# Making the decay matrices' rectified differences during attention and loading them in the state-space stage of a hybrid decoder block

## The chip, the cores and the metric

The kernel runs on one core of a Trainium2 chip. The metric is the device time of one execution in microseconds (us), the median of several runs. The engines are named as in the profile: PE (TensorE, matrix products), PEld (its weight loads), DVE (VectorE), ACT (ScalarE), POOL (GpSimd), SP (SyncE, which issues most DMAs). Each engine takes its own instructions strictly in order; semaphores join the engines.

## The reference

One layer of a hybrid decoder, sequence 1024 with 16 meta tokens ahead, model width 1024. Three mixers read the same normalised input: stick-breaking attention (8 heads of 64), a Mamba-2 state-space mixer (16 heads of 64, state 128) and latent attention (MLA, 8 heads); their joined output is projected and added, and a gated feed-forward layer follows. The change touches the state-space mixer, which works in chunks of 128 tokens:

```python
dA = (dt * a).reshape(b, nc, BLOCK, G, J)
Acs = jnp.cumsum(dA, axis=2)
seg = Acs[:, :, :, None] - Acs[:, :, None, :]
Ldec = jnp.exp(jnp.where(tri[None, None, :, :, None, None], seg, -jnp.inf))
CB = jnp.einsum('bclgn,bcsgn->bclsg', Cc, Bc)
y_diag = jnp.einsum('bclsgj,bcsgjp->bclgjp', CB[..., None] * Ldec, X)
decay = jnp.exp(Acs[:, :, -1:] - Acs)
states = jnp.einsum('bclgn,bclgjp->bcgjpn', Bc, X * decay[..., None])
chunk_decay = jnp.exp(Acs[:, :, -1])
y_off = jnp.einsum('bclgn,bcgjpn->bclgjp', Cc, prev) * jnp.exp(Acs)[..., None]
```

The running sums `Acs` (one number for each token and head) are known long before the state-space stage; everything in the exponentials comes from them alone.

## The kernel before

Activations lie with features on the partitions. Products at full precision are made of three passes (high by high, high by low, low by high parts), lines L145 to L147. Up to about 460 us the kernel does stick-breaking attention in four pairs of heads; beside them, as filler for PE, it makes the next pair's projections and the units of the convolution (`conv_unit`). ACT takes the results out of PSUM (sigmoids `cm`, casts `ph`, `K`, `KS`, `Q`, `cacc`); the two PSUM banks of `d_ps` serve all filler.

In pair 1 the running sums are made (`running_sums`): the product `acum` with a triangular matrix gives `AT` (token on the partition; block and head in the row), and transposed copies are stored in `s_sum` (block, head, token).

The state-space stage (`ssd_chunk`, from about 463 us) goes over 9 chunks (0 is the meta tokens) and in each over two groups `g` of 8 heads. For a group:

- SP loads `R`, the 8 rows of `s_sum`, to all 128 partitions (L786, 512 KB, four buffers).
- ACT makes `cd` (the chunk's whole decay), 8 rectified differences `L = relu(AT - R)` (L795), `ea = exp(R)` in two halves of 64 partitions (L793), and `exp(-L)` (L804). DVE makes `dec` (L789), ACT its exponential (L799).
- POOL scales `X` by `dec` into `Xd` (L800), the state `S` by `cd` (L821), `xs` by the skip gain (L760) and adds `ea` to `y` (L834). DVE multiplies `L` by the masked product `cbm` (L809), `ea` by `yo` (L814), and adds to `S` and `y`.
- PE makes the transpositions `xtp` and `btp`, the products `cbp`, `yo` (old state, L813), `sps` (new state, L817) and `yd` (within the chunk, L829).

Filler for PE there are the units of the latent projections (`latent_units`, L145 to L147), and after these the value projection of MLA (nine blocks, L896 to L898).

What sets the order: the code is written unit by unit, and a list scheduler with its own estimate of durations puts each engine's instructions into one fixed order, in which an instruction that is written later may fill a place that it holds to be free. Buffers come from pools; a tile waits until the earlier user of its buffer is done. `high_priority` and `issue_after` move single blocks.

Of the kernel before, what the change touches and what calls it, by code (L numbers as in the profile page):

```python
# [11 lines left out]
F32 = mybir.dt.float32  # L12
# [47 lines left out]
def tile_hybrid_block(ctx: ExitStack, tc: tile.TileContext, a: dict):  # L60
# [37 lines left out]
    s_v = dram.tile([9, 128, 512], F32, name="s_v")  # L98
    s_sum = dram.tile([9, 16, 128], F32, name="s_sum")
    s_inv = dram.tile([MLA_HEADS, SEQ], F32, name="s_inv")  # L100

# [316 lines left out]

    dx = keep.tile([128, 9 * 16], F32, name="dx")

    def step_sizes():
# [43 lines left out]
    def running_sums(d1):  # L465
        NC = 9 * 16
        pt = tp.tile([128, 512], F32, tag="tp", name="acum")
        pe.matmul(pt[:, :NC], tri, d1, start=True, stop=True)
        dve.tensor_copy(AT.rearrange("p b h -> p (b h)"), pt[:, :NC])

        for i, (t0, n) in enumerate(CH_ALL):
# [5 lines left out]
            act.copy(acs[:, :n], pt[:16, :n])  # L477
            if i == 0:
                sp.dma_start(s_sum[0, :, :META], acs[:, :META])
            nb = min(3, n // 128)  # L480
# [199 lines left out]
    with ctx_sb as st:  # L680
# [20 lines left out]
        pms = meta_tiles(sbb)  # L701

        def sb_attend(p, proj, values):
            Q, K, KS = proj
            for h in range(2):
                for j in range(NQ // 2):
                    rows = [sb_row(Q[h], K[h], KS[h], 2 * j + e) for e in range(2)]
                    weighted_values(tp, pvp, sbb, j, rows, values[0], h, [x[p, 64 * h : 64 * (h + 1)] for x in (s_osbh, s_osbl)], pms[j % 2], values[1])
                    if p == 1 and h == 0 and j == 1:
                        with tc.issue_after(last_on(PE)), tc.issue_after(last_on(DVE)), tc.issue_after(last_on(ACT)):  # L710
                            running_sums(decay_steps())

        values = load_value_steps(sbv, sbb, 0)
# [28 lines left out]
    with ExitStack() as st:  # L742
        la = st.enter_context(tc.tile_pool(name="la", bufs=1, side="right", reuse_waits="tile"))
        p2_st = ExitStack()
        p2 = p2_st.enter_context(tc.tile_pool(name="p2", bufs=2, side="right", reuse_waits="tile"))
        yps = st.enter_context(tc.tile_pool(name="yps", bufs=4, space=PSUM, reuse_waits="tile"))
        dsk = p2.tile([128, 8], F32, bufs=1, name="dsk")
        sp.dma_start(dsk, a["d_skip"])
        S = [p2.tile([128, 512], F32, bufs=1, name=f"S{g}") for g in range(2)]

        def ssd_chunk(c):
# [26 lines left out]
            for g in range(2):  # L778
                gs = slice(512 * g, 512 * (g + 1))
                hs = slice(8 * g, 8 * g + 8)  # L780
                cd = p2.tile([128, 8], F32, tag="cd", name="cd")
                dec = p2.tile([128, 8], F32, tag="dec", name="dec")
                L = p2.tile([128, 8, 128], F32, tag="L", name="L")
                ea = p2.tile([128, 4, 128], F32, tag="yt", bufs=1, name="ea")
                R = p2.tile([128, 8, 128], F32, tag="R", bufs=4, name="R")
                sp.dma_start(R[:, :, :n], s_sum[c, hs, :n].partition_broadcast(128))  # L786
                if c < 8:
                    act.activation(cd, R[:, :, n - 1], AF.Exp)
                    dve.tensor_tensor(dec[:n], R[:n, :, n - 1], AT[:n, c, hs], op=ALU.subtract)  # L789
                if c > 0:  # L790
                    for e in range(2):
                        half = slice(64 * e, 64 * e + 64)
                        act.activation(ea[half], R[half, e::2, :], AF.Exp)  # L793
                    for h in range(8):
                        act.activation(  # L795
                            L[:, h, :], R[:, h, :], AF.Relu, scale=-1.0, bias=AT[:, c, 8 * g + h : 8 * g + h + 1]
                        )
                if c < 8:
                    act.activation(dec[:n], dec[:n], AF.Exp)  # L799
                    pool.tensor_tensor(  # L800
# [958 lines left out]
```

## Time and profile before

| | |
|---|---|
| Median of 3 runs | 1741.38 us (1738.69 to 1743.46) |
| Profiled execution | 1737.8 us, span 1736.0 us |
| PE busy | 1681.3 us (97%) |
| ACT, DVE, POOL busy | 844.6, 1154.7, 735.3 us |
| 213.7 to 285 us (71.3 us): PE, ACT busy | 70.23, 43.65 us |
| 469 to 591 us (122 us): PE, ACT, DVE, POOL busy | 113.35, 98.36, 89.82, 90.32 us |

The span goes from the first to the last instruction of the program. A row of a group gives line, engine, operation, tiles (out<-in), shapes and count; then the busy time in us and the mean of one in ns; then the engine's idle time just before and who ended it. A row with three numbers joined by slashes gives minimum, median and maximum of one in ns. A row of the table by stretches gives start:end, length, then for PE, PEld, DVE, ACT and POOL the busy time with the number of instructions, then the granted clock of TensorE, the DMA engines' share and GB/s.

### The profile page before, as it was taken

The numbers are of one execution on the slowest core, as the hardware profiler recorded it, in microseconds if no ns is written. First come the engines' busy times: TensorE is split into PE (matmuls) and PEld (weight loads), VectorE is DVE, ScalarE is ACT, GpSimd is POOL, SyncE is SP. The second block draws the span as 40 slices with busy tenths as digits, with TensorE's granted clock in tenths as the row PEclk, the third lists the DMA queues.
The fourth block names the chain that finished last, engine by engine and source line by source line (L and its number), as shares of the span: only waits on it lengthen the run. The fifth ranks groups of instructions, "written<-read, shape, count | busy, mean of one in ns | idle before, by whom it ended". The sixth has DMA issues, their size and how long they took to land.

```text
span 1736.0 us, 26095 instructions
## 1 busy us (share of the span) xinstructions
PE 1681.3 (97%) x9529; PEld 1471.2 (85%) x9529; DVE 1154.7 (67%) x1726; ACT 844.6 (49%) x1763; POOL 735.3 (42%) x525
## 2 busy tenths in 40 slices
PE   8899999999998999999999999999999999999998
PEld 7889999999987789998888878778888888878887
DVE  7677568778587544556576556966666666688644
ACT  7465466556577627776454325422222322343333
POOL 3544335243578447563231445635554555200012
PEclk9999999999999999999999999999999999999999
DMA  4222222122566655348222352222322233999602
GB/s 164 72 73 66 82 81 88 39 83 71 173 213 170 211 203 153 113 122 285 62 80 75 94 178 73 71 100 92 113 93 97 93 101 110 329 395 370 234 1 97
DMA packets 150133, 230.90 MB, mean 133 GB/s; under 512 B 27043, under 2 KB 86597, under 8 KB 150005
## 3 DMA queue, kind: packets, MB, share of 16 engines
q1 hardware_dynamic: 130608, 213.67, 38.1%
q10 hardware_dynamic: 19396, 15.56, 3.0%
q8 instruction: 75, 1.23, 0.3%
q14 instruction: 54, 0.43, 0.1%
HBM read 166.07 MB, written 63.10 MB: 132 GB/s over the span
## 4 chain that ended last, share of the span: by engine, by line
PE 72%; DVE 7%; DMA 6%; issue 2%; POOL 2%; ACT 1%; SPq 1%; DVEq 0%; ACTq 0%; POOLq 0%
PE d_ps L145 8%; PE d_ps L147 8%; PE d_ps L146 8%; PE b_ps L1269 7%; PE b_ps L1271 7%; PE b_ps L1270 7%; PE b_ps L1554 2%; PE b_ps L1555 2%; PE b_ps L1553 2%; PE ptg L326 2%; DMA raw<-in_w_down_dram 1%; PE pv L305 1%; PE ptg L328 1%; PE pv L304 1%; PE sc_ps L979 1%
## 5 line engine op out<-in xcount | busy, mean ns | idle before, releaser
L145 PE MATMUL d_ps<-hnh,whi 128*128 128x384 f32 (+6 forms) x744 | 246.5, 331 | 3.6 <-DVE KS L607 2.4
L147 PE MATMUL d_ps<-hnl,whi 128*128 128x384 f32 (+6 forms) x744 | 246.6, 331 | 0.0
L146 PE MATMUL d_ps<-hnh,wlo 128*128 128x384 f32 (+6 forms) x744 | 245.8, 330 | 0.0
L134 POOL TENSOR_TENSOR wlo<-wraw,whi 128x1024 fp32r<-128x1024 f32 (+1 forms) x57 | 137.3, 2408 | 200.7 <-ACT whi L132 200.2
L145 PEld LDWEIGHTS d_ps<-hnh,whi 128*128 128x128 f32 (+1 forms) x744 | 140.1, 188 | 7.8 <-ACT vs L582 1.7
L147 PEld LDWEIGHTS d_ps<-hnl,whi 128*128 128x128 f32 (+1 forms) x744 | 140.1, 188 | 3.1 <-issue 0.8
L146 PEld LDWEIGHTS d_ps<-hnh,wlo 128*128 128x128 f32 (+1 forms) x744 | 140.1, 188 | 2.3
L1270 PE MATMUL b_ps<-T,wl 128*128 128x512 f32 x352 | 139.1, 395 | 1.3 <-POOL wl L1101 1.3
L1271 PE MATMUL b_ps<-T,wh 128*128 128x512 f32 x352 | 138.7, 395 | 1.3 <-DVE T L1101 1.3
L1269 PE MATMUL b_ps<-T,wh 128*128 128x512 f32 x352 | 139.1, 396 | 0.0
L312 DVE TENSOR_TENSOR pl<-ptg,ph 128x512 fp32r<-128x512 f32 (+1 forms) x160 | 99.8, 628 | 53.1 <-ACT ph L311 51.9
L696 DVE TENSOR_TENSOR_SCAN cm<-cm,sb_mask 128x144 f32<-128x144 f32 (+3 forms) x64 | 107.5, 1687 | 29.1 <-issue 18.8
L1100 ACT CAST op<-raw 128x1024 fp32r<-128x1024 f32 x69 | 71.1, 1050 | 110.3 <-PE d_ps L1555 65.4
L1101 DVE TENSOR_TENSOR op<-raw,op 128x1024 fp32r<-128x1024 f32 x69 | 84.1, 1229 | 40.5 <-ACT op L1100 40.4
L311 ACT CAST ph<-ptg 128x512 fp32r<-128x512 f32 (+1 forms) x160 | 85.6, 542 | 44.2 <-PE ptg L328 23.4
L132 ACT CAST whi<-wraw 128x1024 fp32r<-128x1024 f32 (+1 forms) x57 | 58.8, 1032 | 68.8 <-PE d_ps L147 35.1
L1101 POOL TENSOR_TENSOR wlo<-raw,whi 128x1024 fp32r<-128x1024 f32 x18 | 45.0, 2499 | 109.7 <-ACT whi L1100 109.7
L1101 POOL TENSOR_TENSOR wl<-raw,wh 128x512 fp32r<-128x512 f32 x46 | 75.5, 1648 | 30.2 <-ACT wh L1100 30.2
L1107 POOL TENSOR_TENSOR tt<-tt 128x512 f32<-128x512 f32 (+1 forms) x8 | 8.1, 1015 | 187.6 <-ACT tt L1625 187.4
L1104 DVE TENSOR_TENSOR raw<-raw 128x512 f32<-128x512 f32 x58 | 58.5, 1016 | 42.0 <-DMA raw<-in_w_gate_dram 37.3
L1100 ACT CAST wh<-raw 128x512 fp32r<-128x512 f32 x88 | 53.2, 616 | 65.9 <-PE b_ps L1271 65.8
L1270 PEld LDWEIGHTS b_ps<-T,wl 128*128 128x128 f32 x352 | 66.5, 189 | 17.3 <-POOL wl L1101 1.6
(431 smaller groups left out, 5117.8 us busy)
## 6 DMA issues: line engine op xcount, KB each, us to landing
raw<-in_w_down_dram SPq DMA_DIRECT2D x99, 256.0 KB, 5.3
s_hops<-gs SPq DMA_DIRECT2D x63, 256.0 KB, 2.0
raw<-s_hops SPq DMA_DIRECT2D x63, 256.0 KB, 5.4
raw<-in_w_gate_dram SPq DMA_DIRECT2D x22, 512.0 KB, 3.7
raw<-in_w_up_dram SPq DMA_DIRECT2D x22, 512.0 KB, 4.3
R<-s_sum SPq DMA_DIRECT2D x16, 512.0 KB, 4.7
wraw<-in_w_o_dram SPq DMA_DIRECT2D x16, 512.0 KB, 3.7
wraw<-in_w_xbc_dram SPq DMA_DIRECT2D x12, 512.0 KB, 4.0
```

The source lines that it names most:

```text
L134: pool.tensor_tensor(lo[:, :cols], raw[:, :cols], f32(hi[:, :cols]), op=ALU.subtract)
L145: pe.matmul(ps[:m, :n], wh, mh, start=(kt == 0), stop=False)
L146: pe.matmul(ps[:m, :n], wl, mh, start=False, stop=False)
L147: pe.matmul(ps[:m, :n], wh, ml, start=False, stop=(kt == nkt - 1))
L311: act.copy(ph[:, :n], pt[:, :n])
L312: dve.tensor_tensor(pl[:, :n], pt[:, :n], f32(ph[:, :n]), op=ALU.subtract)
L696: dve.tensor_tensor_scan(rev, rev, sb_mask[:, T - n_all :][:, ::-1], 1.0, ALU.mult, ALU.max)
L1100: act.copy(hi, value)
L1101: eng.tensor_tensor(lo, value, f32(hi), op=ALU.subtract)
L1269: pe.matmul(banks[j], hi[:, ks], UH[u][k], start=start and k == 0, stop=False, skip_group_check=skip)
L1270: pe.matmul(banks[j], lo[:, ks], UH[u][k], start=False, stop=False, skip_group_check=skip)
L1271: pe.matmul(banks[j], hi[:, ks], UL[u][k], start=False, stop=stop and k == 3, skip_group_check=skip)
```

## The change

For each chunk but the meta one and each group a function `differences` loads the 8 rows of `s_sum` to all partitions, makes the 8 rectified differences in place (`rel`, two buffers) and stores them in a new DRAM tensor `s_rel` (16 x 512 KB). It is called in the attention of pairs 2 and 3, once after each query step. The state-space stage loads `L` from `s_rel` (four buffers instead of two) and has no `R` any more; it loads the rows for `ea` a second time, by themselves (two loads of 128 KB for a group), and makes their exponential in one instruction over 128 partitions. `cd` and `dec` no longer come from `R`: `running_sums` makes the blocks' whole sums by two more products, subtracts `AT`, and a single exponential at the start of the stage (`decay`) makes all of both. The meta block's sums aren't stored any more. A scratch region for DMA descriptors is halved from 4096 to 2048.

```diff
+    SUMS = keep.tile([128, 2, 9 * 16], F32, name="SUMS")
...
+        pt = tp.tile([128, 512], F32, tag="tp", name="asum")
+        pe.matmul(pt[:, :16], ones[:META], d1[:META, :16], start=True, stop=True)
+        pe.matmul(pt[:, 16:NC], ones, d1[:, 16:], start=True, stop=True)
+        dve.tensor_copy(SUMS[:, 0], pt[:, :NC])
+        pool.memset(SUMS[:, 1, :16], 0.0)
+        for rows, c in ((slice(0, META), slice(0, 16)), (slice(0, 128), slice(16, NC))):
+            dve.tensor_tensor(
+                SUMS[rows, 1, c], SUMS[rows, 0, c], AT.rearrange("p b h -> p (b h)")[rows, c], op=ALU.subtract
+            )
...
-            if i == 0:
-                sp.dma_start(s_sum[0, :, :META], acs[:, :META])
...
+        def differences(c, g):
+            d = sbb.tile([128, 8, 128], F32, tag="rel", name="rel")
+            sp.dma_start(d, s_sum[c, 8 * g : 8 * g + 8].partition_broadcast(128))
+            for h in range(8):
+                act.activation(
+                    d[:, h, :], d[:, h, :], AF.Relu, scale=-1.0, bias=AT[:, c, 8 * g + h : 8 * g + h + 1]
+                )
+            sp.dma_start(s_rel[c - 1, g], d.rearrange("p h t -> p (h t)"))
...
+                    if p > 1:
+                        differences(4 * (p - 2) + j + 1, h)
...
+        decay = p2.tile([128, 2, 9, 16], F32, bufs=1, name="decay")
+        act.activation(decay.rearrange("p e b h -> p e (b h)"), SUMS, AF.Exp)
...
-                cd = p2.tile([128, 8], F32, tag="cd", name="cd")
-                dec = p2.tile([128, 8], F32, tag="dec", name="dec")
-                L = p2.tile([128, 8, 128], F32, tag="L", name="L")
-                ea = p2.tile([128, 4, 128], F32, tag="yt", bufs=1, name="ea")
-                R = p2.tile([128, 8, 128], F32, tag="R", bufs=4, name="R")
-                sp.dma_start(R[:, :, :n], s_sum[c, hs, :n].partition_broadcast(128))
-                if c < 8:
-                    act.activation(cd, R[:, :, n - 1], AF.Exp)
-                    dve.tensor_tensor(dec[:n], R[:n, :, n - 1], AT[:n, c, hs], op=ALU.subtract)
+                cd, dec = decay[:, 0, c, hs], decay[:, 1, c, hs]
                 if c > 0:
+                    L = p2.tile([128, 8, 128], F32, tag="L", bufs=4, name="L")
+                    ea = p2.tile([128, 4, 128], F32, tag="yt", name="ea")
+                    sp.dma_start(L.rearrange("p h t -> p (h t)"), s_rel[c - 1, g])
                     for e in range(2):
                         half = slice(64 * e, 64 * e + 64)
-                        act.activation(ea[half], R[half, e::2, :], AF.Exp)
-                    for h in range(8):
-                        act.activation(
-                            L[:, h, :], R[:, h, :], AF.Relu, scale=-1.0, bias=AT[:, c, 8 * g + h : 8 * g + h + 1]
-                        )
+                        sp.dma_start(ea[half], s_sum[c, 8 * g + e : 8 * g + 8 : 2].partition_broadcast(64))
+                    act.activation(ea, ea, AF.Exp)
                 if c < 8:
-                    act.activation(dec[:n], dec[:n], AF.Exp)
```

How the fixed order of instructions changes, at three places.

ACT in attention, just after the running sums, before (`acs` are the transposed running sums, `pm` and `ph` casts of attention weights, `K` and `KS` of keys, `whi` of weights):

```order
L318 CAST pm<-ptm 16x256
L311 CAST ph<-ptg 128x512
L132 CAST whi<-wraw 128x1024
L311 CAST ph<-ptg 128x512
L604 CAST K<-d_ps 64x272
L605 CAST KS<-d_ps 64x272
L694 ACT_TABLE_LOAD
```

and now (line numbers of the changed kernel):

```order
L319 CAST pm<-ptm 16x256
L312 CAST ph<-ptg 128x512
L716 ACTIVATE rel<-rel,AT 128x128 x8
L312 CAST ph<-ptg 128x512
L613 CAST K<-d_ps 64x272
L614 CAST KS<-d_ps 64x272
L133 CAST whi<-wraw 128x1024
L703 ACT_TABLE_LOAD
```

The first lot of eight differences stands here, in pair 1, and the other fifteen follow it; the last lot stands so, among the results of the convolution:

```order
L501 ACTIVATE cacc<-d_ps,cb,cw 128x272
L716 ACTIVATE rel<-rel,AT 128x128 x8
L319 CAST pm<-ptm 16x256
L501 ACTIVATE cacc<-d_ps,cb,cw 128x384
L512 ACTIVATE csig<-cacc 128x272
```

That `cacc` is the one that starts at 285.7 us in the trace of before. Between the first and the last lot stand 91 other instructions of ACT.

SP between the stores of the running sums and the first conv weights, now (`rel<-s_sum` is the load of a lot, `s_rel<-rel` its store; the load of `w_sbq` before stood right behind the stores of `s_sum`):

```order
L491 DMA s_sum<-acs 16x2x128
L491 DMA s_sum<-acs 16x3x128
L714 DMA rel<-s_sum 128x1024
L491 DMA s_sum<-acs 16x3x128
L131 DMA wraw<-in_w_sbq_dram 128x1024
L404 DMA vlast<-s_vsb 64x8x1 x4
```

and some 20 rows on:

```order
L714 DMA rel<-s_sum 128x1024
L131 DMA wraw<-in_w_xbc_dram 128x1024
L719 DMA s_rel<-rel 128x1024 x2
L714 DMA rel<-s_sum 128x1024 x2
L719 DMA s_rel<-rel 128x1024 x2
L714 DMA rel<-s_sum 128x1024 x2
L131 DMA wraw<-in_w_xbc_dram 128x1024
```

Loads and stores of the two `rel` buffers stand in turn in the one queue of SP, with the weights of the next unit behind them.

PE at the end of the state-space stage, before (all nine blocks of the value projection stand ahead of the last `yd`):

```order
L896 MATMUL d_ps<-whi,lhi 128x512
L897 MATMUL d_ps<-whi,llo 128x512
L898 MATMUL d_ps<-wlo,lhi 128x512
L829 MATMUL yd<-L,X 64x128 x8
L145 MATMUL d_ps<-lhi,whi 128x272
```

and now (the meta block, 16x512, and one of the others stand ahead of it, seven behind):

```order
L909 MATMUL d_ps<-whi,lhi 128x512
L910 MATMUL d_ps<-whi,llo 128x512
L911 MATMUL d_ps<-wlo,lhi 128x512
L842 MATMUL yd<-L,X 64x128 x8
L826 MATMUL yo<-bc,S_5597 128x128 x4
L842 MATMUL yd<-L,X 64x128 x8
L909 MATMUL d_ps<-whi,lhi 128x512
L910 MATMUL d_ps<-whi,llo 128x512
```

At the stage's other end, 24 filler products of 128x384 that stood ahead of the first `xtp` now stand behind it.

More of the change, by code (lines that the diff above doesn't have):

```diff
@@ L99, in tile_hybrid_block @@
     s_sum = dram.tile([9, 16, 128], F32, name="s_sum")
+    s_rel = dram.tile([8, 2, 128, 1024], F32, name="s_rel")
     s_inv = dram.tile([MLA_HEADS, SEQ], F32, name="s_inv")
@@ L1747 @@
     }
-    nc = bacc.Bacc("TRN2", target_bir_lowering=False, num_devices=1, dynamic_dma_scratch_size=4096)
+    nc = bacc.Bacc("TRN2", target_bir_lowering=False, num_devices=1, dynamic_dma_scratch_size=2048)
     aps = {
```

## The prediction

> **What bounds the kernel now.** The page first: TensorE (PE) is busy for 97% of the span, no other engine for more than 67%, and in the chain that ended last it holds 72%.
>
> ```profile
> span 1736.0 us, 26095 instructions
> PE 1681.3 (97%) x9529; PEld 1471.2 (85%) x9529; DVE 1154.7 (67%) x1726; ACT 844.6 (49%) x1763; POOL 735.3 (42%) x525
> PE 72%; DVE 7%; DMA 6%; issue 2%; POOL 2%; ACT 1%; SPq 1%; DVEq 0%; ACTq 0%; POOLq 0%
> ```
>
> So an edit pays only where PE waits, and it costs wherever it makes PE wait. Next the table by stretches, for the two stages that the change touches (each engine's busy time with its instructions in brackets, then granted clock, DMA share, GB/s):
>
> ```profile
> 213.70:285.00 71.30, 70.23 (x467) 66.57 (x467) 50.36 (x75) 43.65 (x96) 27.16 (x21) 1.00 0.28 79
> 300.00:340.00 40.00, 40.00 (x251) 37.27 (x250) 28.52 (x40) 22.63 (x54) 12.85 (x7) 1.00 0.20 59
> 340.00:380.00 40.00, 40.00 (x276) 39.13 (x275) 30.19 (x47) 23.68 (x53) 17.99 (x14) 1.00 0.24 70
> 469.00:591.00 122.00, 113.35 (x828) 93.15 (x826) 89.82 (x118) 98.36 (x249) 90.32 (x66) 0.97 0.65 201
> 469.00:480.00 11.00, 9.99 (x74) 9.45 (x71) 5.66 (x11) 8.16 (x28) 6.42 (x5) 1.00 1.05 371
> 480.00:591.00 111.00, 103.36 (x755) 83.70 (x755) 84.16 (x108) 90.20 (x222) 83.90 (x61) 0.97 0.61 184
> ```
>
> Attention (213 to 460 us) is PE's own: busy 40.00 of 40, weight loads (PEld) 37 to 39 of 40. The state-space stage, 122 us from its first transposition to its last product, is not: PE is busy for 113.35 but its weight loads for only 93.15 (76%), because matmuls overlap and a busy PE hides short waits. There ACT (98.36), POOL (90.32) and DVE (89.82) are all at three quarters or more. If weight loads stood as dense as in attention, the stage would last about 93.15/0.97 = 96 us; some 26 us is the most that it can give back.
>
> **What leaves the state-space stage.** Groups by line:
>
> ```profile
> L795 ACT ACTIVATE L<-R,AT 128x128 f32<-128x128 f32 x128 | 39.4, 388 | 1.6 <-PE yd L829 1.6
> L793 ACT ACTIVATE ea<-R 64x512 f32<-64x512 f32 x32 | 20.0, 625 | 1.3 <-POOL y L834 1.1
> L788 ACT ACTIVATE cd<-R 128x8 f32<-128x8 f32 x16 | 3.3, 209 | 2.9 <-POOL S L821 1.6 <-DMA R<-s_sum 1.0
> L799 ACT ACTIVATE dec<-dec 128x8 f32<-128x8 f32 (+1 forms) x16 | 3.2, 204 | 15.4 <-DVE dec L789 15.4
> L789 DVE TENSOR_TENSOR dec<-R,AT x16: 147/840/1039, 470.8 to 558.3; 128x8 f32<-128x8 f32 x14, 16x8 f32<-16x8 f32 x2
> ```
>
> The 128 rectified differences (39.4 us; 0.31 us apiece when they follow each other), the small exponentials (3.3 + 3.2) and half of `ea` go: 16 of 128x512 instead of 32 of 64x512, the same 512 columns, so 16 x 0.625 = 10.0 instead of 20.0. ACT falls by 39.4 + 10 + 6.5 = 56, from 98 to 42 us. DVE loses `dec`, 10.7 us, and ACT its 15.4 us wait for it.
>
> **What stays** is POOL's chain and DVE's long product (minimum/median/maximum ns):
>
> ```profile
> L809 DVE TENSOR_TENSOR L<-L,cbm x16: 1207/1969/3451, 483.0 to 586.8; 128x1024 f32<-128x1024 f32 x16
> L834 POOL TENSOR_TENSOR y<-y,ea x16: 1266/1286/2267, 490.9 to 590.2; 128x512 f32<-128x512 f32 x16
> L821 POOL TENSOR_TENSOR S<-S,cd x14: 1037/1048/2041, 488.2 to 582.1; 128x512 f32<-128x512 f32 x14
> L800 POOL TENSOR_TENSOR Xd<-X,dec x16: 1034/1046/2024, 473.6 to 566.4; 128x512 f32<-128x512 f32 x14, 16x512 f32<-16x512 f32 x2
> L760 POOL TENSOR_TENSOR y<-xs,dsk x8: 1897/1898/1933, 471.8 to 580.2; 128x1024 f32<-128x1024 f32 x8
> ```
>
> An 8-column DVE subtraction takes 147 ns at best and 840 at the median, L809 1.21 and 1.97 us, and POOL's L821 now and then double: DVE operations with both inputs in SBUF and POOL's take turns. At the minima POOL's four lines are 20.3 + 14.5 + 16.5 + 15.2 = 66.5 us, L809 19.3, `dec` 2.4; with POOL's other work here, 90.32 less the four lines' busy 74.7, or 15.6, that is 104 us of taking turns in 122 (85%). Without `dec` 101 remain, so the stage can't get under about 101. I take 111 us, about midway between that and the 119 at which the turns would again be 85% full, because the second crowded engine (ACT) is gone: 11 us off the stage, from 3 to 21. [...]
>
> The DMA side is a smaller brake. The new `ea` loads add 16 x 256 KB = 4.2 MB; 184 GB/s at a share of 0.61 is 302 GB/s when full, so they are 14 us of all DMA engines on top of 0.65 x 122 = 79: 93 in 111. It holds, with longer landings, and is a reason not to take less than 111.
>
> **Not all 11 us count.** Products of other units fill PE in this stage, and the order of the change puts fewer among them: 24 products of 128x384 that stood ahead of the first transposition now follow it, and of the nine blocks of the value projection (six products of 128x512 each, L896 to L898) that all stood ahead of the last `yd`, seven follow it: 42 products. Their pace:
>
> ```profile
> 457.00:463.00 6.00, 6.00 (x36) 6.00 (x35) 0.42 (x1) 2.03 (x5) 1.75 (x2) 1.00 0.65 157
> 1200.00:1240.00 40.00, 40.00 (x173) 32.31 (x173) 26.11 (x31) 11.85 (x19) 20.09 (x13) 1.00 0.31 99
> ```
>
> 6.00/36 = 0.17 us for 384 columns, 40/173 = 0.23 for 512. The stage starts 24 x 0.17 = 4.1 us earlier in PE's work and leaves 42 x 0.23 = 9.7 us for later, 5.6 net. It gives back 11 - 5.6 = 5.4 us.
>
> **What attention has to take.** The 128 differences do not spread over the last two pairs. On ACT the order puts them between the cast `ph` at 213.7 us and the accumulator `cacc` at 285.7, in 16 lots of eight, with about 90 of ACT's other instructions between. In those 71.3 us ACT is busy for 43.65 (row above); 39.4 more makes 83.05, an overload of 11.75 us even if ACT never waited. PE needs ACT for every bank that it fills (casts of K, Q and `ph`, sigmoids, `cacc`), and engines work in order, so what ACT is late by reaches PE, less PE's lead. More is added by the loads and stores of `rel`:
>
> ```profile
> DMA to landing us min/median/max: 3.5/4.6/5.7
> wraw<-in_w_xbc_dram SPq DMA_DIRECT2D x3, 512.0 KB, 3.9
> s_y<-y ACTq DMA_DIRECT2D x7, 512.0 KB, 3.5
> 218.00 1.05 ACT L132 CAST whi<-wraw 128x1024 fp32r<-128x1024 f32 x1 [3.67 <-DMA wraw<-in_w_sbq_dram]
> ```
>
> The first line is the same broadcast of 512 KB in the state-space stage (`R`), the second a load of that size in attention, the third a store of it. `rel` has two buffers, so each turns once per load 4.1 + eight differences 2.5 + store 3.5 + issues 0.7 = 10.8 us: 5.4 per lot, 86 us for 16. ACT's own pace is 83.05/16 = 5.2 per lot. Two rings of equal pace, joined in order, hold each other up: I add 5 us, between 0 (ACT always finds its lot landed) and 15 (about one per lot). The first lot has to wait for the running sums to be stored and read back; ACT stood idle there anyway for 3.67 us, so 1 more. The load waits on SP, and behind it stand the queries' weights (the `whi` above waits for them), and later the conv weights and the stores of `csig`; on ACT a lot whose load is late holds the casts behind it, for which PE waits. Both are in the 5. PE's lead takes off 3, between 0 and 6: two banks of 24 products of 0.17 us. The two sums by matmul, three DVE operations and a memset are 0.5 (0 to 1.5): they follow the copy of `AT` in DVE's queue and nothing reads them before the state-space stage. Attention: 11.75 + 5 + 1 - 3 + 0.5 = 15 us, between 6 and 28. It isn't won back, for PE has no idle time behind it until 465.
>
> Costed at nothing: the loads of `L`, which have the size of those of `R`, and four buffers as these had. They are freed later, by `yd` instead of the differences, still two chunks ahead. If that cover went, a landing of 4.6 us per lot would show. The skipped store of the meta block's sums and the smaller scratch are free too.
>
> **Sum** against the profiled execution: 15 - 5.4 = +9.6 us, span 1745.6. That execution took 1737.8, 3.6 below the median of 1741.38, so the median should be about 1751.
>
> **Rivals.**
>
> 1. *Attention has room.* The scheduler placed the lots where ACT idles, some of them in real gaps (3.67 us at 214), PE's lead takes the rest, and attention loses only 4. The stage, free of ACT, comes near its floor: 104 us. Then 4 - 18 + 5.6 = -8.4: 1733. For it: ACT at 61% in these 71 us, its largest single holder gone from a stage where it was the busiest. Against: 83 us of work in 71. It is faster from the point where attention loses less than the stage's saving over 5.6.
> 2. *The two `rel` buffers bind.* If a store takes until the next lot is due each time (15 for the rings, no lead of PE: 28 + 1), attention loses 29: 29 - 5.4 = +23.6: 1765. For: equal paces, SP in order. Against: DMA share only 0.28 there.
> 3. *The turns of DVE and POOL bind.* The stage stays 85% full of them and lasts 119: 15 - 3 + 5.6 = +17.6: 1759. [...] For: 104 of 122. Against: ACT was as full, and DVE waits for it too.
>
> That the change does not do what it says: the differences stand beside the second pair rather than the last two, which is already in the sum.
>
> **Chances.** Forecast 0.47, first rival 0.30, second 0.10, third 0.13. About 0.3% (5.2 us) is what a measurement can tell. Slower by more: 0.34 of the forecast's share and both late rivals, 0.57; faster by more: 0.25 of the first rival's; the rest, 0.18, within. The forecast's own range is 1742 to 1762; to leave out no more than 2 in 10 it has to take in the first rival and most of the second: 1731 to 1766.
>
> **What would show it.** In attention: PE busy below 60 of the 71 us that follow the running sums, ACT at 95% or more there, PE and DVE waiting for ACT (`ph`, `K`, `cacc`), the first `xtp` near 469 - 4 + 15 = 480 us. In the state-space stage: ACT near 42 us busy, first `xtp` to last `yd` 111 us, L809's median still well above 1.2 us. Wrong if PE stays full beside the differences, or if the stage shortens by 18 or more; the DMA share near 0.85 in the stage would show the loads, and waits of ACT for `rel<-s_sum` the second rival.

## The result, and the profile after

| | Before | Changed |
|---|---|---|
| Median | 1742.42 us (4 runs) | 1766.56 us (4 runs) |
| Ratio, with 95% interval | | 1.0149 [1.0134, 1.0163] |
| Span of the profiled execution | 1736.0 us | 1763.6 us |

The change makes the kernel 1.5% slower: about 24 us by the medians, 27.6 by the spans. The forecast was 1751 with a range to 1766: right in its sign, with less than half of the size, and the time lies 0.6 us outside the range. First the page of the changed kernel (span, the engines' busy times, the chain that ended last):

```profile
span 1763.6 us, 26167 instructions
PE 1695.6 (96%) x9533; PEld 1481.2 (84%) x9533; DVE 1137.7 (65%) x1713; ACT 829.6 (47%) x1716; POOL 730.1 (41%) x526
PE 71%; DMA 9%; DVE 8%; ACT 3%; issue 3%; POOL 2%; SPq 1%; DVEq 0%; ACTq 0%; POOLq 0%
```

PE is busy for 96.1% of the span instead of 96.8%, and DMA has 9% of the chain instead of 6%. Then the tables by stretches, before and after, cut at the product `acum` (running sums), at the first `xtp` and at the last `yd`. Columns: start:end, length, PE, PEld, DVE, ACT, POOL busy with the number of instructions, granted clock, DMA share, GB/s. Before:

```profile
208.00:469.10 261.10, 259.83 (x1739) 249.66 (x1738) 184.59 (x259) 156.05 (x346) 110.49 (x81) 1.00 0.28 80
469.10:590.60 121.50, 112.85 (x824) 92.72 (x822) 89.72 (x118) 97.96 (x249) 89.82 (x66) 0.97 0.65 201
```

and after (the second and third rows are parts of the first: the stretch with the lots, and ten microseconds of it):

```profile
206.20:489.10 282.90, 268.03 (x1718) 253.75 (x1717) 183.87 (x262) 190.70 (x472) 105.10 (x79) 0.96 0.43 132
218.00:315.00 97.00, 82.90 (x463) 75.52 (x462) 51.81 (x75) 79.41 (x221) 29.21 (x22) 0.89 0.68 221
225.10:235.30 10.20, 8.51 (x29) 7.77 (x30) 7.18 (x10) 10.01 (x30) 3.90 (x4) 0.50 0.67 250
489.10:608.80 119.70, 111.34 (x807) 92.03 (x806) 73.96 (x102) 43.73 (x70) 92.95 (x67) 0.93 0.77 228
```

**Attention** takes 21.8 us longer with 21 products fewer in it (3.6 us at 0.17): some 25 us lost. The lots, which the order had put beside 71 us of the kernel before, take 97 us, and PE's 463 products there cover 82.90 of them. PE's time without work in attention (length less busy time) grows from 1.3 to 14.9 us. On top of that the granted clock is 0.89 in the 97 us with the lots; in the row of 10.2 us it is 0.50.

**The state-space stage** is 1.8 us shorter, with 17 products fewer. ACT's busy time has gone from 97.96 to 43.73 us as forecast, and nothing came of it. What ACT waited for there, before (line, releaser, us in total, times, longest):

```profile
ACT dec L799 <- DVE dec L789: 15.4, 9, 4.1
ACT cd L788 <- POOL S L821: 1.6, 2, 1.4
```

and after:

```profile
ACT ea L811 <- DMA ea<-s_sum: 32.9, 14, 6.0
ACT L L817 <- DMA L<-s_rel: 25.0, 11, 4.2
```

Where ACT worked it now waits for loads, 58 us in all, and what stands behind a waiting instruction on ACT comes late with it. One such place, ACT in order of time, where `btok` starts at 496.87 us behind waits of 4.03 and 0.67 us:

```profile
494.60 1.06 ACT L817 ACTIVATE L<-L 128x1024 f32<-128x1024 f32 x1 [4.03 <-DMA L<-s_rel]
496.33 0.63 ACT L811 ACTIVATE ea<-ea 128x512 f32<-128x512 f32 x1 [0.67 <-DMA ea<-s_sum]
496.87 0.34 ACT L799 COPY btok<-btp 16x256 f32<-16x256 f32 x1
```

PE's waits in this stage, largest three:

```profile
PE sps L830 <- POOL Xd L813: 3.6, 2, 2.3
PE xtp L790 <- ACT btok L799: 2.3, 1, 2.3
PE d_ps L175 <- ACT lrow L755: 1.0, 1, 1.0
```

`btok` needs no load, but stands behind `L` and `ea`; the second row is PE waiting 2.3 us for it, just behind the place above, and the clock halves at 498.2 us for 6.8 us.

**After the stage** the kernel takes 9.4 us more (1154.8 for 1145.4), for the 42 products of the value projection that follow now.

For all kernels one more measure is used, worked out from the traces. For each form of PE product the lower quartile of its step (start to next start) in the trace of before is taken as its unhindered pace; the length of a stretch less the paces of its products is what the stretch was *held up*. It sets off products moved in or out. Before, attention (`acum` to first `xtp`) is held up by 16.4 us and the stage by 32.6; after, by 41.8 and 36.2; what lies behind the stage as much after as before, within 1 us. So in these two executions attention lost 25.4, the stage 3.6.

### The profile page after: what moved, and what is told of

Its sections match the earlier page's. It is cut to its first block, busy times and chain, and to the rows that moved or that the text cites. A ratio compares the mean times of both kernels' runs of the same rounds, so it can differ in the third digit from the quotient of the medians.

```text
span 1763.6 us, 26167 instructions
## 1 busy us (share of the span) xinstructions
PE 1695.6 (96%) x9533; PEld 1481.2 (84%) x9533; DVE 1137.7 (65%) x1713; ACT 829.6 (47%) x1716; POOL 730.1 (41%) x526
## 4 chain that ended last, share of the span: by engine, by line
PE 71%; DMA 9%; DVE 8%; ACT 3%; issue 3%; POOL 2%; SPq 1%; DVEq 0%; ACTq 0%; POOLq 0%
PE d_ps L146 8%; PE d_ps L148 8%; PE d_ps L147 8%; PE b_ps L1283 7%; PE b_ps L1284 7%; PE b_ps L1282 7%; PE b_ps L1567 2%; PE b_ps L1568 2%; PE b_ps L1566 2%; PE ptg L327 2%; DMA rel<-s_sum 2%; DMA s_rel<-rel 1%; PE ptg L329 1%; DMA raw<-in_w_down_dram 1%; PE pv L306 1%
## 5 line engine op out<-in xcount | busy, mean ns | idle before, releaser
L146 PE MATMUL d_ps<-hnh,whi 128*128 128x384 f32 (+6 forms) x744 | 251.1, 337 | 4.8 <-DVE KS L616 3.9
L1114 DVE TENSOR_TENSOR op<-raw,op 128x1024 fp32r<-128x1024 f32 x69 | 84.9, 1239 | 41.8 <-ACT op L1113 40.2
```

Of the source, the lines that this page charges most:

```text
L146: pe.matmul(ps[:m, :n], wh, mh, start=(kt == 0), stop=False)
L1114: eng.tensor_tensor(lo, value, f32(hi), op=ALU.subtract)
```

## The experiments

| Kernel | Median, us | Ratio to before, 95% | Attention held up | Stage, us / products / held up |
|---|---|---|---|---|
| before | 1742.42 | | 16.4 | 121.5 / 824 / 32.6 |
| changed | 1766.56 | 1.0149 [1.0134, 1.0163] | 41.8 | 119.7 / 807 / 36.2 |
| e1 four ea buffers | 1768.04 | 1.0160 [1.0135, 1.0185] | 42.6 | 118.7 / 803 / 36.2 |
| e2 lots spread | 1741.46 | 1.0009 [0.9994, 1.0024] | 22.9 | 114.8 / 786 / 31.3 |
| e3 attention part alone | 1756.88 | 1.0092 [1.0061, 1.0124] | 37.9 | 114.4 / 824 / 25.8 |
| e4 block sums alone | 1735.83 | 0.9964 [0.9950, 0.9978] | 19.4 | 117.1 / 843 / 25.3 |
| e5 no loads in the stage | 1755.62 | 1.0091 [1.0063, 1.0120] | 43.7 | 104.8 / 805 / 20.3 |
| e6 no ea loads | 1759.40 | 1.0107 [1.0085, 1.0129] | 43.6 | 108.3 / 817 / 22.1 |
| e7 no differences | 1752.62 | 1.0058 [1.0034, 1.0081] | 23.7 | 116.4 / 775 / 34.4 |
| e8 no loads of rel | 1750.72 | 1.0058 [1.0036, 1.0080] | 34.6 | 110.6 / 810 / 25.4 |
| e9 long packets | 1769.40 | 1.0172 [1.0149, 1.0195] | 50.7 | 114.6 / 829 / 25.7 |
| e10 spread, long packets | 1742.68 | 1.0016 [1.0002, 1.0031] | 18.7 | 113.2 / 752 / 35.6 |
| e11 the same, four ea buffers | 1743.26 | 1.0015 [1.0003, 1.0026] | 17.2 | 113.2 / 763 / 33.8 |
| e12 e11, latent units held back | 1759.16 | 1.0112 [1.0090, 1.0134] | 39.2 | 119.9 / 854 / 28.5 |
| e13 e4, latent units held back | 1755.53 | 1.0085 [1.0068, 1.0102] | 32.0 | 124.7 / 876 / 29.5 |
| e14 before, latent units held back | 1759.26 | 1.0104 [1.0086, 1.0121] | 33.0 | 123.7 / 860 / 31.4 |
| e15 e11, held from the seventh | 1746.11 | 1.0048 [1.0031, 1.0065] | 31.5 | 112.3 / 820 / 24.8 |
| e16 e11, held from the eighth | 1749.83 | 1.0055 [1.0035, 1.0075] | 29.6 | 116.2 / 808 / 30.1 |
| e17 e11, held in two steps | 1741.33 | 1.0003 [0.9991, 1.0015] | 22.0 | 112.5 / 806 / 27.7 |
| e18 the same, one chunk less | 1744.05 | 1.0017 [1.0005, 1.0030] | 25.5 | 117.4 / 816 / 31.4 |

Each ratio is to the kernel before as timed in the same series (its medians there are 1740.2 to 1742.4). The right columns come from one profiled execution each. The stage of kernels whose stage is the same code (in e7 but for one sign) still differs by several us (121.5 before, 114.4 in e3; 119.7, 116.4 and 110.6 in the changed kernel, e7 and e8), so differences in the stage below about 9 us, or 11 of what is held up, are no evidence by themselves.

**e1: four buffers for ea.** In the changed kernel the loads of `ea` wait on SP until POOL's `y` has freed one of two buffers (37.1 us in 12 waits), and SP holds the loads behind them: it issues nothing from 500.1 to 512.8 us, then two loads of `ea`, and only then the next `L`.

```diff
-                    ea = p2.tile([128, 4, 128], F32, tag="yt", name="ea")
+                    ea = p2.tile([128, 4, 128], F32, tag="yt", bufs=4, name="ea")
```

> The changed kernel with four buffers instead of two for ea in the state-space stage, nothing else. Theory (the ring of two ea buffers holds the stage): in the changed kernel the loads of ea waited on SP for POOL's addition y two groups earlier, up to 12 us, with the loads of L and xs behind them, and ACT then stood 33 us for ea and 25 for L; with four buffers these waits fall under 10 us each, the stage shortens from 119.7 to about 108 us, and the time falls from 1766.6 to about 1755. Rival (DMA bandwidth or the turns of DVE and POOL hold it): the loads are issued earlier but land as late, or POOL stays the bound; stage 117 to 120, time 1764 to 1768.

Nothing gained, as the rival said. ACT's waits moved from one load to the other:

```profile
ACT L L817 <- DMA L<-s_rel: 33.4, 13, 5.7
ACT ea L811 <- DMA ea<-s_sum: 15.0, 10, 4.8
```

The ring of `ea` buffers is not the cause here; that theory fell.

**e2: the lots spread over pairs 2 and 3.**

```diff
-                        differences(4 * (p - 2) + j + 1, h)
+                        with tc.issue_after(last_on(PE)), tc.issue_after(last_on(DVE)), tc.issue_after(last_on(ACT)):
+                            differences(4 * (p - 2) + j + 1, h)
```

> The changed kernel with each of the sixteen lots of differences ordered behind the PE, DVE and ACT instructions that stand ahead of its call, so that the lots lie one after each query step of pairs 2 and 3, instead of packed into 100 us. Theory (packing: more work than ACT has room for, and loads that come too late, and a slower PE clock after each wait): attention loses under 5 us instead of 24, PE stays over 98% busy with granted clock 1.00 there, time about 1746. Rival (each lot costs wherever it stands: 2.5 us of ACT in one piece hold the casts behind it and eat PE's lead, about 1 us each): attention loses 16 us, time about 1758.

1741.5: the packing was the loss, all 25 us by the medians. The same 128 differences now lie between 298 and 476 us, and attention is held up by 6.5 us more than before instead of 25.4, a little over the 5 expected:

```profile
208.10:486.30 278.20, 272.63 (x1811) 262.02 (x1810) 180.35 (x264) 196.37 (x480) 111.42 (x83) 0.99 0.44 141
```

**e3: the attention part alone**, on the kernel before: `differences` and its call as in the change (and the smaller scratch), the result not used.

```diff
+                    if p > 1:
+                        differences(4 * (p - 2) + j + 1, h)
```

> The kernel before, which makes and stores the differences in attention as the change does, but does not use them: the state-space stage still loads R and makes everything there. Theory (the whole loss is attention's, the new stage gives nothing back but costs little): about 1742 + 24 = 1766, the same as the changed kernel. Rival (the new stage is itself slower by what its loads hold up): attention alone costs 12 to 18, time 1754 to 1760. If the new stage did give back as forecast (5 us), this kernel would be at 1771.

1756.9, +16 us by the median: the rival's number. By it the rest of the change, the new stage, costs about 10, where it was to give back 5. The profiled execution (1752.1 us, the fastest of its four) shows attention held up by 21.5 more and the unchanged stage by chance 7 less; so how the loss divides between attention and the stage (16 and 10 by the medians, 25 and 4 by the profiles) is known only to within 5 to 10 us. That the stage gives nothing back both say.

**e4: the block sums alone**, on the kernel before: `SUMS` and `decay` as in the change (also the store and the row load of the meta block, which fall away, and the smaller scratch); `R`, the differences and `ea` stay.

```diff
-                    act.activation(cd, R[:, :, n - 1], AF.Exp)
-                    dve.tensor_tensor(dec[:n], R[:n, :, n - 1], AT[:n, c, hs], op=ALU.subtract)
+                cd, dec = decay[:, 0, c, hs], decay[:, 1, c, hs]
```

> The kernel before with the change's block sums alone: cd and dec of all blocks from one exponential at the start of the stage; R, the differences and ea stay in the stage, nothing is added to attention. Theory (ACT's 15 us wait for dec on DVE, 6.5 us of small exponentials and 10.7 us of DVE subtraction stood in the stage's chain): the stage shortens by 6 us or more, time about 1736. Rival (the turns of DVE and POOL and the loads set the stage, ACT has slack): stage within 2 us of 121.5, time 1740 to 1744.

1735.8, ratio 0.9964 [0.9950, 0.9978]: the theory's time, and the only kernel here that is faster than the one before. The stage is 4.4 us shorter with 19 products more in it. ACT is nearly as busy there as before (95.02 for 97.96 us); what went is its wait of 15.4 us for `dec`, and DVE's subtractions (78.36 us busy for 89.72). Which of the two makes the gain was not separated:

```profile
467.50:584.60 117.10, 113.11 (x843) 92.76 (x842) 78.36 (x104) 95.02 (x220) 96.82 (x67) 1.00 0.68 211
```

**e5 and e6: without loads in the stage.** e5 loads one tile of differences and one of rows for `ea` and uses them for all groups; e6 does so for `ea` alone.

```diff
-                    sp.dma_start(L.rearrange("p h t -> p (h t)"), s_rel[c - 1, g])
...
-                        sp.dma_start(ea[half], s_sum[c, 8 * g + e : 8 * g + 8 : 2].partition_broadcast(64))
-                    act.activation(ea, ea, AF.Exp)
+                    act.activation(ea, ea0, AF.Exp)
...
-                    act.activation(L, L, AF.Exp, scale=-1.0)
+                    act.activation(L, L0, AF.Exp, scale=-1.0)
```

> The changed kernel without the loads of L and ea in the state-space stage: one tile of differences and one of rows for ea are loaded once at its start, and all sixteen groups take their exponentials from these (what y holds is then another number; every other instruction stays). Theory (the loads come late, ACT stands before them, and btok, lrow and vtok, for which PE waits, stand behind on ACT): ACT's 58 us of waiting for L and ea vanish, the stage falls from 119.7 to about 105 us, time about 1752. Rival (the turns of DVE and POOL set the stage's length): the stage stays at 115 us or more, time 1762 to 1767.

> The changed kernel with the loads of L as they are, but the rows for ea loaded once and used by all sixteen groups (y holds another number). Theory (the added loads of ea, 4.2 MB, are what makes all loads late, since those of L have the size that R had): most of what the kernel without any loads gains, time 1752 to 1757. Rival (the loads of L are late by themselves, since their buffers come free only after the last product of the group): little gained, 1762 to 1767.

The stage of e5, from the table by stretches:

```profile
496.10:600.90 104.80, 103.92 (x805) 85.79 (x803) 74.14 (x101) 39.96 (x66) 92.42 (x66) 1.00 0.48 142
```

and that of e6:

```profile
493.00:601.30 108.30, 107.17 (x817) 89.87 (x817) 72.70 (x101) 43.88 (x69) 93.05 (x67) 0.98 0.69 217
```

Without loads the stage lasts 104.8 us for nearly the same products (805 for 807), and PE's waits there fall from 8.4 to 0.9 us. DVE and POOL do the same work in 104.8 us as in 119.7 (74.14 and 92.42 us busy). So the turns of DVE and POOL did not set the stage's length; the loads did. The medians are 11 (e5) and 7 us (e6) below the changed kernel, and the interval of neither touches that of the changed kernel. That `ea` makes most of it (32 loads of 256 pieces of 512 B) is likely but not shown: the intervals of e5 and e6 overlap, and 1759.4 lies between what theory and rival of e6 had said. Without the loads of `ea` the share of the DMA engines falls from 0.77 to 0.69, and ACT still waits for `L` in e6:

```profile
ACT L L817 <- DMA L<-s_rel: 23.9, 12, 4.0
```

So ACT's waits for `L` by themselves do little harm here. The sum of ACT's waits is not the price of the loads at all: in e15 below, whose stage is held up by 24.8 us only, they are 54 us, nearly the 58 of the changed kernel.

```profile
ACT L L830 <- DMA L<-s_rel: 37.4, 15, 6.6
ACT ea L824 <- DMA ea<-s_sum: 16.9, 10, 2.8
```

A wait must count by what stands behind it for PE, like `btok` above; the traces show that in single places, not as a sum.

**e7 and e8: the two halves of attention's loss.** e7 leaves out the 128 differences, e8 the loads of `rel`.

```diff
-            for h in range(8):
-                act.activation(
-                    d[:, h, :], d[:, h, :], AF.Relu, scale=-1.0, bias=AT[:, c, 8 * g + h : 8 * g + h + 1]
-                )
```

```diff
-            sp.dma_start(d, s_sum[c, 8 * g : 8 * g + 8].partition_broadcast(128))
...
-                    d[:, h, :], d[:, h, :], AF.Relu, scale=-1.0, bias=AT[:, c, 8 * g + h : 8 * g + h + 1]
+                    d[:, h, :], sb_mask[:, :128], AF.Relu, scale=-1.0, bias=AT[:, c, 8 * g + h : 8 * g + h + 1]
```

> The changed kernel with its loads and stores of rel in attention, but without the 128 differences on ACT (the rows of sums are stored as they are, and their exponential is taken without the minus; y holds another number). Theory (ACT's overload makes attention's loss, the transfers little): attention loses under 6 us instead of 24, time about 1747. Rival (the transfers and what they hold up on SP make it): attention loses 12 us or more, time 1755 or more.

> The changed kernel with the 128 differences on ACT and their stores, but taken from a constant tile instead of the loaded rows, so that none waits for a load (y holds another number). Theory (ACT's overload makes attention's loss: 39.4 us of work where 28 are free): attention loses 12 to 18 us, time 1755 to 1761. Rival (late loads, the ring of two buffers, make it): attention loses under 8 us, time 1747 to 1751.

Attention is held up by 23.7 us in e7 (7.3 more than before) and by 34.6 in e8 (18.2 more). The two sum to 25.5; the whole lost 25.4. So in attention's own stretch ACT's work makes 18 of the 25 and the transfers make 7, nearer to the overload theory. In e8 the lots lie within 70 us, and ACT is full there while PE is not:

```profile
209.80:279.90 70.10, 58.03 (x337) 51.80 (x336) 31.13 (x48) 67.28 (x194) 17.85 (x14) 0.93 0.51 175
```

The medians don't separate the two: they lie 14 (e7) and 16 us (e8) below the changed kernel. That of e7, 1752.6, falls between its theory and its rival, and that of e8 is the rival's number. In e8's profiled execution the stage too was 9 us shorter than after (110.6), which no edit of it explains, and e7's was not.

**e9: long packets.** `s_sum` is stored in the order in which `ea` takes it.

```diff
-                        sp.dma_start(ea[half], s_sum[c, 8 * g + e : 8 * g + 8 : 2].partition_broadcast(64))
+                        sp.dma_start(ea[half], s_sum[c, g, e].partition_broadcast(64))
...
-            sp.dma_start(s_sum[3 * i + 3 - nb : 3 * i + 3].rearrange("b h t -> h b t"), src)
+            for g in range(2):
+                for e in range(2):
+                    sp.dma_start(
+                        s_sum[3 * i + 3 - nb : 3 * i + 3, g, e].rearrange("b j t -> j b t"),
+                        src[8 * g + e : 8 * g + 8 : 2],
+                    )
```

> The changed kernel with the rows of s_sum stored in the order in which ea takes them (group, even heads, odd heads), so that each partition's 2 KB of an ea load lie in one piece: 2048 packets of 2 KB instead of 8192 of 512 B, the same bytes. The stores of the running sums become four small ones each, and the order of heads inside rel and L follows. Theory (the ea loads cost by their packets, and hold SP and the transfers behind them): the stage falls from 119.7 us toward the 108 of the kernel without ea loads, 110 to 113, time about 1758. Rival (their waiting for POOL's addition, or the bytes, are what counts): stage 117 or more, time 1764 to 1768.

The time, 1769.4, is that of no gain, even above the rival's. In the profile the stage is held up by 25.7 us instead of 36.2, a difference that executions of one stage show too, and attention by 50.7 instead of 41.8. The stores of the sums, three before, are twelve now:

```profile
L719 SPq DMA_DIRECT2D rel<-s_sum x16: 319/320/1216, 224.8 to 325.4; - x16
L493 SPq DMA_DIRECT2D s_sum<-acs x12: 589/591/769, 212.2 to 219.5; - x12
```

At 0.59 us each they hold SP for 7 us, and the first load of `rel` goes out at 224.8 us instead of 211.9.

**e10 and e11: spread lots with long packets**, e11 with four `ea` buffers as well.

> The lots of differences spread over pairs 2 and 3 (as in the kernel that came out at 1741.5 us), together with the long packets for ea. If the long packets shorten the stage by 6 us or more, time about 1735, below the kernel before by about 0.3% and level with the kernel with block sums alone (1735.8). If they don't, 1740 to 1743.

> The same with four buffers for ea. Theory (with short transfers, the wait for POOL's addition is what is left of the lateness): 2 to 4 us below the kernel with two, about 1732. Rival (as with long transfers, where four buffers changed nothing): the same within 2 us.

No gain over e2, although attention is now held up by only 1 to 2 us more than before. In the traces 106 products more than before stand ahead of the stage, and fewer in it: 752 and 763. PE waits 12.5 and 8.8 us in the stage, which lasts 113 us all the same; in e15 and e17 it lasts 112 with 820 and 806 products.

**e12 to e18: the filler given back.** The products of the latent units are ordered behind the first transposition of the stage: all of them in e12 (on e11), e13 (on e4) and e14 (on the kernel before), some in e15 and e16. In e17 and e18 some wait for attention's last product and the others for the first transposition.

```diff
-            dense_fm(dpool, load_w(w[u]), KT, 128, mov, chunks, evac)
+            wu = load_w(w[u])
+            with tc.issue_after(began[0]):
+                dense_fm(dpool, wu, KT, 128, mov, chunks, evac)
```

> Lots spread over pairs 2 and 3, long packets and four buffers for ea, and the products of the latent units held back until the first transposition of the state-space stage, so that PE has them to fill its waits there (620 products in the order's stage where the kernel without holding had 521 and the kernel before 578). Theory (the stage is a chain of loads, POOL and DVE of about 113 us, whatever PE does beside it; its gain shows only as other work put in): the stage stays near 115 us with 100 products more, 17 us of PE's work, and the time falls from 1743 to about 1732. Rival (the filler delays the chain as much as it fills): the stage grows by 15 us, time 1740 to 1745.

> The kernel before with the block sums alone, and the latent units held back in the same way (642 products in the order's stage). Theory: its stage of 117 us has little room left, PE waits there for 4 us only; time 1731 to 1736. Rival (too much filler in one place): slower, 1738 or more.

> The kernel before with the latent units held back alone. Theory (the stage of the kernel before has 8.6 us of waiting of PE and 3.4 us of lost clock to be filled): 1734 to 1739. If holding alone is worth nothing there, 1741 within 2 us, and what the other two gain comes from the decay's edits.

> Lots spread, long packets, four ea buffers; of the latent units the chunks from the seventh on are held back until the first transposition of the state-space stage, so that the order's stage has 578 products, as many as in the kernel before. Theory (the chain of the stage is shorter, PE's filler was missing): stage 112 us against 121.5, attention 2 to 5 us more, time 1731 to 1737. Rival (attention's cost and the stage's gain cancel whatever the filler): 1739 to 1743.

> The same, with the chunks from the eighth on held back (566 products in the order's stage). Theory and rival as for the seventh: 1731 to 1737, or 1739 to 1743; that both agree within 3 us would show that the exact split matters little.

> Lots spread, long packets, four ea buffers; of the latent units' chunks the first four are free, the fifth to seventh wait for attention's last product and the others for the first transposition of the state-space stage. The order then has 2935 products up to attention's end, 78 between it and the stage, 560 in the stage (the kernel before: 2944, 67, 578). Theory (the stage is 9 us shorter at equal filler, attention costs 3 to 5): time 1733 to 1738. Rival (what the stage gains, attention and the stage's start lose whatever the split): 1740 to 1745.

> The same with the first three chunks free and the fourth to sixth behind attention's last product (2911, 78 and 571 products). Theory and rival as for e17: 1733 to 1738, or 1740 to 1745.

Holding all back costs 15 to 20 us in whichever kernel (e12 and e14 are equal). That fits e13's rival (slower) and lies outside every range given for e12 and e14. These products also fill PE while the stage's first loads arrive; without them PE stands 7 to 9 us there. In e12, e13 and e14, in this order:

```profile
PE xtp L800 <- DMA xs<-s_xs: 9.3, 1, 9.3
PE xtp L782 <- DMA xs<-s_xs: 8.3, 1, 8.3
PE xtp L772 <- DMA xs<-s_xs: 7.2, 1, 7.2
```

In e15, where six chunks run early and none waits at attention's end, the wait is longer: PE stands 13.1 us before the first transposition, and the granted clock over that time is 0.53.

```profile
PE xtp L802 <- DMA xs<-s_xs: 13.1, 1, 13.1
```

The same time and the stage behind it, by stretches:

```profile
467.80:480.90 13.10, 0.04 (x1) 0.07 (x2) 5.98 (x7) 6.49 (x12) 2.38 (x2) 0.53 0.82 231
480.90:593.20 112.30, 109.04 (x820) 90.81 (x820) 72.88 (x99) 43.07 (x69) 86.30 (x64) 0.98 0.81 239
```

The last row is its stage: 112.3 us for 820 products. With that gap filled (e17) the stage is held up 4.9 us less than before and attention 5.6 more, and the time is that of the kernel before, ratio 1.0003 [0.9991, 1.0015]. e15 and e16 (1746.1 and 1749.8) are slower than both their ranges; e17 and e18 came out as their rivals said. So with everything repaired that the experiments had found, the whole change is worth nothing, while its block sums alone (e4) are worth 5 us: moving the differences costs about what the block sums gain.

## Why the prediction was wrong, step by step

The sum had 15 us for attention and took 5.4 off for the stage and its filler. By the profiles attention lost 25.4 and the stage 3.6, so two steps failed, each by 9 to 10 us: the stage's gain, and a term that attention's sum did not have, the clock. The medians of e3 also say that the stage gave nothing back (it cost 10); by them attention's 15 was met (16), so the second failure rests on the profiles alone.

**The order's packing: right.** All 16 lots stood beside what had taken 71 us, and PE waited for ACT there. ACT's wait for the loads and PE's two largest waits for ACT in the changed kernel between 218 and 315 us:

```profile
ACT rel L716 <- DMA rel<-s_sum: 16.8, 9, 5.5
PE pv L305 <- ACT ph L312: 4.5, 4, 1.4
PE sc_ps L701 <- ACT cm L703: 3.7, 2, 1.8
```

e2 shows that the packing, not the amount of work, made the loss.

**Overload 11.75, less a lead of 3: too small.** With ACT's work alone (e8) PE was without work in attention for 12.2 us more (13.5 against 1.3 before), about 3.5 more than 11.75 less 3. That PE's lead took nothing off is one reading; the 2.8 us that ACT stood idle in the row of e8 above can have added nearly as much. The sign "ACT at 95% or more" held in e8 (67.28 of 70.10 us); in the changed kernel ACT was busy for 79.41 of 97 us and waited 16.8 for the loads.

**Rings and first load, 5 + 1: too large as waits, about right as a price.** The whole less e8 is 7.2 us, and e7 alone gives 7.3. But only 1.4 of it is more waiting of PE (14.9 for 13.5 us); about 5 is clock.

**The clock: no term.** All of PE's added waiting in attention is 13.6 us, near the 15 of the sum. What the sum left out is that the clock was at half rate for 20.5 us beside these waits, 10.2 us of lost work (in e8 5.1, before none).

**"It isn't won back": right.** Behind the stage the kernel was held up as much as before.

**The stage, 111 us: wrong.** The step that failed is "because the second crowded engine (ACT) is gone", with "the DMA side is a smaller brake". ACT's work was not what the stage waited for: with 54 us less of it, the stage was 119.7. The new loads, estimated at 14 us of the DMA engines and costed as a reason not to take less than 111, took the gain: without them 104.8 (e5), without those of `ea` alone 108.3 (e6). As a sum for the DMA engines the estimate was good: 93 us were forecast, and a share of 0.77 of 119.7 us is 92. It went wrong in asking only whether the engines have room: no wait for these loads, and for what stands behind the waiting instruction, was in the sum. Later landings of the other loads don't explain it. The traces tell those of `xs` for only one to three of the seven loads in each of these kernels; the medians before, in the changed kernel and in e6:

```profile
xs<-s_xs SPq DMA_DIRECT2D x7, 512.0 KB, 3.8
xs<-s_xs SPq DMA_DIRECT2D x7, 512.0 KB, 6.1
xs<-s_xs SPq DMA_DIRECT2D x7, 512.0 KB, 5.9
```

In e6 they come as late as in the changed kernel, and the stage is 11 us shorter. Through which waits the loads of `ea` cost PE its time stays open. Costing the loads of `L` "at nothing" was part of the same step; e6, which keeps them with 23.9 us of ACT's waiting, is only 3.5 us longer in the stage than e5, so that size was nearly right.

**Less filler in the stage: right.** 42 products behind it were costed at 9.7 us; the part after the stage grew by 9.4.

**The rivals.** The second gave 1765, which the time came near by luck: it had full rings (29 us in attention, a stage of 111), and the transfers made 7. The third gave a stage of 119 through the turns of DVE and POOL; the length came out so, by another cause: e5 keeps their work and lasts 104.8, not far above the 101 us that the forecast had estimated as the floor that the turns leave. Single instructions show the turns: in the changed kernel DVE's product with `cbm` takes 1.35 to 2.15 us in the twelve places where POOL works on 512 columns or more for over 0.2 us after its start, and 1.22 in the other four. But they did not decide the time. The first rival's floor of 104 for the stage was met only without loads. No rival held both halves: an attention that loses 25 and a stage that gives nothing.

**What stays open:** why single executions of the same stage differ by up to 9 us, how the loads reach PE, and whether long packets really shorten the stage (25.7 us held up in e9, 24.8 and 27.7 in e15 and e17, but 31.4 in e18 and 35.6 in e10). That four `ea` buffers matter with long packets was not separated either.

## What to carry to other kernels

Work moved to an emptier engine has to be spread by the order, not by the totals: 39 us of ACT, with their loads and stores, held attention up by 1 to 7 us when spread over 160 to 180 us of it, and by 25 when put beside what had taken 71. When computation is replaced by a load, look at when it lands and at what stands behind the waiting instruction on its engine, not at the busy time saved alone. Where PE's waits are summed, add a term for the clock that they cost (in the changed kernel's attention 10.2 us of work beside 13.6 us of added waiting). And take a change apart before judging it: its least part, the block sums, gained 0.36% [0.22%, 0.50%] by itself, while the whole lost 1.5%.

## What the runs showed of the hardware that was not expected

**A short wait of PE often cost more than its length.** In the changed kernel the clock was granted at half rate for 20.5 us of attention, always beside a wait: the row of 10.2 us at 0.50 above follows waits of 0.8, 0.3 and 1.8 us. The half-rate stretches of the traces before and after, between 100 and 1700 us, last 3.41, 6.83 or 10.24 us. Over the 20 traces of this study, between 100 and 1700 us, a half-rate stretch began during a wait of PE or within 2 us of its end in 64 of 86 waits of 2 us or more, in 38 of 70 of 1.5 to 2 us, in 24 of 154 of 1 to 1.5 us, and in 19 of 414 shorter ones. Of the waits of 2 to 2.5 us two thirds (27 of 41) had such a stretch, and at 3.41 us the shortest takes 1.7 us of work (half of it).

**One issue on SP took 1.8 times as long as another, and not by its bytes.** In the changed kernel the issue of a load of `ea` (128 KB, 64 partitions) takes 0.607 us at the median (the first line is of the tile `ea`), that of a load of `L` (512 KB, 128 partitions) 0.338:

```profile
L810 SPq DMA_DIRECT2D ea<-s_sum x32: 574/607/1301, 488.2 to 602.5; - x32
```

```profile
L807 SPq DMA_DIRECT2D L<-s_rel x15: 319/338/775, 489.7 to 589.9; - x15
```

With a quarter of the pieces (e9) the first came to 0.546, so the count of pieces is only part of it; what else was not isolated. The twelve small stores of e9 took 0.591 each.
